# Stacked keys and doubled queries in the attention scores of one hybrid decoder layer, narrow key tiles with both heads in one bank, and a norm's mean placed between two projection tiles

## The chip, the cores and the metric

The kernel runs on one core of one Trainium2 chip. A core has five engines that work side by side, each through its own list of instructions, in order: PE (TensorE) multiplies matrices, DVE (VectorE) and ACT (ScalarE) work elementwise, POOL (GpSimd) does the same more slowly, and SP (SyncE) starts data transfers (DMAs). They wait for each other by semaphores. PE writes its results into PSUM, a small memory of eight banks of 128 partitions by 512 f32 values; everything else lies in SBUF, 128 partitions wide. The metric is the device time of one execution in microseconds; the lower the better.

## The reference

One layer of a decoder over 512 tokens of width 1024, in f32. What matters here is the first sublayer. From h = RMSNorm(x) one projection makes q, k, v (8 heads of 64), the inputs of a short convolution, and two gates. The heads do a causal "stick-breaking" attention:

```python
z = einsum('bhqd,bhkd->bhqk', qb, kb) / sqrt(64)          # scores
log_fail  = where(k_pos < q_pos, log_sigmoid(-z), 0)
log_later = cumsum(log_fail, reverse, over keys) - log_fail
weights   = where(k_pos < q_pos, exp(log_sigmoid(z) + log_later), 0)
out       = einsum('bhqk,bhkd->bhqd', weights, vb)
```

The convolution branch and the attention branch are projected, gated, added and projected again (x1 = x + ...). Then a cross-attention from RMSNorm(x1) into 256 memory tokens (4 heads of 256, softmax), then a SwiGLU feed-forward of width 2816, then a last norm.

## The kernel before, in words

Activations are held transposed (features on partitions, the 512 tokens along the row). Every f32 operand of a product is split into two parts of TensorE's f32r type, hi (a rounded copy, made by ACT) and lo (the rest, made by DVE: source minus hi). A product is three matmuls, hi*hi, hi*lo and lo*hi, added up in one PSUM bank (`mm3`, L153; the instructions of a projection carry the lines L154 to L156). A projection of 128 output features is 24 such matmuls of 512 columns (`gemm`, L158); the weights come through `load_w` (L137): SP loads 512 KB (`wr`), ACT makes `wh` (L149), DVE makes `wl` (L150), four buffers of each.

The attention runs over `steps`: four pairs of heads p, and in each the key tiles kt = 3, 2, 1, 0. A tile holds 128 keys on partitions and the queries that can see them along the row: `span(kt)` gives n = 256 columns for kt = 3 and kt = 2, 384 for kt = 1, 512 for kt = 0. One step has three parts, which the loop at L448 interleaves: `scores` of the next step, `weights` of this one and `values` of the one before.

- `qk_part` (L283) projects one of q and k for a pair of heads, scales it on DVE (L286, tile `qk`) and splits it (`split`, L168 and L169): head 0 on partitions 0 to 63, head 1 on 64 to 127.
- `scores` (L348): for each head its own PSUM bank z; three matmuls per head whose operands are 64 partitions high (L356), the two heads alternating. Then, per head, three ACT passes (L361 to L363: abs, exp, ln), one on DVE (L364), the causal mask on POOL (`causal`, L336), a split (`lsplit`, L344 and L345) and for kt of 2 and 1 the running sum over later keys (L373) and a second split.
- `weights` (L377): matmuls add the later keys' sums (L385, a matrix of -1) and the sums within the tile (L388, a triangle of -1) onto z in PSUM; ACT takes exp (L390), POOL masks, DVE makes the two parts `ah` and `al` (L394, L395).
- `values` (L399): four matmuls with v (L406). Here v is stored as hi in one half of the 128 columns and lo in the other, so two matmuls per head do.

Around these lies the `fill`: projections of the next heads, of the convolution and of the first gates, handed out over the 16 steps. Nothing in the code fixes the order within this stage on an engine: the framework orders the instructions of each engine from their priorities and a cost model when the program is built.

Later, at L605, the residual x1 is made with the sum of its squares (`squares_mean`, L176). `mean1[1]` (`turned`, L193) turns that sum into one reciprocal root per token: two matmuls with a matrix of 1/1024 (L185, tile `varb`), an ACT copy of one row (L196, `vrow`), two small DMAs that lay it out over partitions (L205, L207, `vr`), and six small operations (`rstd_of`, L116). The cross-attention's queries are `mem_q(h)` (L613), two projections of 24 matmuls (`mq`), made from the not yet normed x1 so that the mean isn't needed for them; `r1s` (L625) enters the softmax scale.

## Time and profile before

| | us |
|---|---|
| median of 3 runs (lowest, highest) | 860.55 (859.35, 860.62) |
| the profiled execution's own time | 860.42 |
| its span, first to last instruction | 858.7 |
| what lies around the span | 1.7 |

The stages along the span, by the trace: to 27 us the load of x and the projection of v; 27 to 207 us the attention with its fill; to 311 us gates and branches; to 356 us the memory's keys and values; to 400 us x1; to 463 us, overlapping, the cross-attention; to 516 us its output; 517 to 747 us the first and 747 to 843 us the second half of the feed-forward; then the last norm and the stores.

How the rows are read: a row of the timeline is start, length, engine, line, operation, output<-inputs, shapes, how many (x); brackets give the idle time before it and what ended that. Matmuls of PE overlap in their pipeline, so a length of 0.39 us is not the pace: the pace is the distance from one start to the next. A row x2 merges instructions that follow each other.

### The profile page before, as it was taken

The page shows a single profiled execution, that of the slowest core. Times are in us where ns is not written, and L with a number is a line of the kernel's source. Part 1 is how long each engine was busy: PE and PEld are TensorE (multiplying, and loading weights), DVE is VectorE, ACT ScalarE, POOL GpSimd, SP SyncE. Part 2 cuts the span into 40 slices and gives each one's busy share as a digit, 9 for nine tenths or more (in the row PEclk, how much of TensorE's full clock was granted, in tenths as well). Part 3 has the DMA queues.
Part 4 walks back from the last instruction along what each step waited for, and adds up shares of the span by engine and source line. Part 5 has one row for each costly group of instructions (what it writes and reads, how often), then busy time and mean ns, then how long its engine had stood idle before and what let it go on. Part 6 is the DMA issues. An engine that isn't in the chain of part 4 may idle for free.

```text
span 858.7 us, 12803 instructions
## 1 busy us (share of the span) xinstructions
PE 844.8 (98%) x4822; PEld 735.7 (86%) x4822; DVE 657.7 (77%) x1074; ACT 459.7 (54%) x843; POOL 153.7 (18%) x187
## 2 busy tenths in 40 slices
PE   9999999999999999999999999999999999999995
PEld 7788888877888899887888789999999999888884
DVE  7778888987665766577455678888888778999886
ACT  7466676665332354443444565655444555576654
POOL 0022221111566630064000011111111110000001
PEclk9999999999999999999999999999999999999998
DMA  8422212224578765466341325676676763465452
GB/s 295 138 96 86 87 63 73 74 75 172 217 284 305 285 235 193 172 245 241 107 130 50 92 69 148 175 191 175 182 186 178 189 187 88 155 224 199 163 179 98
DMA packets 49232, 139.55 MB, mean 163 GB/s; under 512 B 5265, under 2 KB 7313, under 8 KB 46354
## 3 DMA queue, kind: packets, MB, share of 16 engines
q1 hardware_dynamic: 39538, 103.83, 35.0%
q0 software_dynamic: 9344, 34.62, 15.4%
q8 instruction: 38, 0.62, 0.3%
q10 hardware_dynamic: 288, 0.28, 0.1%
q14 instruction: 24, 0.20, 0.1%
HBM read 125.07 MB, written 13.64 MB: 162 GB/s over the span
## 4 chain that ended last, share of the span: by engine, by line
PE 95%; DVE 3%; ACT 1%; issue 1%; POOL 0%; ACTq 0%; POOLq 0%
PE z L738 15%; PE p L1001 10%; PE pr L155 8%; PE pr L156 8%; PE pr L154 8%; PE y L738 7%; PE v L738 4%; PE r L154 3%; PE r L155 3%; PE r L156 3%; PE v L267 3%; PE br L154 2%; PE br L155 2%; PE br L156 2%; PE mq L156 2%; PE mq L154 2%
## 5 line engine op out<-in xcount | busy, mean ns | idle before, releaser
L149 ACT CAST wh<-wr 128x1024 fp32r<-128x1024 f32 x84 | 88.0, 1052 | 163.9 <-issue 71.2
L150 DVE TENSOR_TENSOR wl<-wr,wh 128x1024 fp32r<-128x1024 f32 x84 | 110.6, 1319 | 35.5 <-ACT wh L149 35.5
L155 PE MATMUL pr<-xgl,wh 128*128 128x512 f32 x288 | 112.4, 390 | 0.0
L156 PE MATMUL pr<-xgh,wl 128*128 128x512 f32 x288 | 112.3, 390 | 0.0
L154 PE MATMUL pr<-xgh,wh 128*128 128x512 f32 x288 | 112.2, 390 | 0.0
L478 POOL TENSOR_TENSOR pre<-pre 128x512 f32<-128x512 f32 x44 | 71.8, 1636 | 31.7 <-DMA pre<-in_w_ffn_out_dram 29.4
L707 POOL DMA_DIRECT2D ws<-in_w_ffn_in_dram x22 | 26.6, 1207 | 260.9 <-DVE wf L728 104.1
L738 PE MATMUL z<-xdh,wf 128*128 128x256 f32 x352 | 70.4, 283 | 0.2 <-ACT sb L759 0.2
L156 PEld LDWEIGHTS pr<-xgh,wl 128*128 128x128 f32 x288 | 54.1, 188 | 11.3
L154 PEld LDWEIGHTS pr<-xgh,wh 128*128 128x128 f32 x288 | 54.1, 188 | 11.1
L155 PEld LDWEIGHTS pr<-xgl,wh 128*128 128x128 f32 x288 | 54.1, 188 | 11.0
L759 ACT COPY sa<-z 128x256 f32<-128x256 f32 x44 | 16.4, 373 | 79.0 <-PE z L738 78.1
L738 PEld LDWEIGHTS z<-xdh,wf 128*128 128x128 f32 x352 | 57.9, 192 | 0.5 <-ACT sb L759 0.4
L728 DVE TENSOR_TENSOR wf<-s,wf 128x512 fp32r<-128x512 f32 x44 | 30.3, 691 | 25.8 <-ACT wf L727 25.7
L738 PE MATMUL z<-xdl,wf 128*128 128x256 f32 x176 | 49.8, 283 | 0.0
L819 DVE TENSOR_TENSOR wl<-wr,wh 128x1024 fp32r<-128x1024 f32 x33 | 40.3, 1220 | 5.1 <-ACT wh L886 5.1
L886 ACT CAST wh<-wr 128x1024 fp32r<-128x1024 f32 x33 | 34.6, 1049 | 5.7 <-ACT f01h L815 2.4
L738 PE MATMUL z<-xch,wf 128*128 128x256 f32 x176 | 35.4, 284 | 0.1
L738 PE MATMUL y<-xch,wf 128*128 128x256 f32 x176 | 35.4, 283 | 0.0
L738 PE MATMUL v<-xoh,wf 128*128 128x256 f32 x176 | 35.4, 283 | 0.0
L738 PE MATMUL z<-xf,wf 128*128 128x256 f32 x264 | 35.4, 283 | 0.0
L738 PE MATMUL y<-xoh,wf 128*128 128x256 f32 x176 | 35.3, 283 | 0.0
(332 smaller groups left out, 2417.0 us busy)
## 6 DMA issues: line engine op xcount, KB each, us to landing
wr<-in_w_in_dram SPq DMA_DIRECT2D x36, 512.0 KB, 3.3
pre<-in_w_ffn_out_dram POOLq DMA_DIRECT2D x11, 1024.0 KB, 8.2
sums<-pre POOLq DMA_DIRECT2D x11, 1024.0 KB, 5.1
ws<-in_w_ffn_in_dram SPq DMA_DIRECT2D x22, 512.0 KB, 3.7
wg<-in_w_ffn_in_dram SPq DMA_DIRECT2D x22, 512.0 KB, 4.1
ws<-in_w_ffn_in_dram POOLq DMA_DIRECT2D x22, 512.0 KB, 5.9
wr<-sums SPq DMA_DIRECT2D x22, 512.0 KB, 3.9
wr<-in_w_ffn_out_dram SPq DMA_DIRECT2D x16, 512.0 KB, 4.0
```

The source lines that it names most:

```text
L149: after(nc.scalar.copy(h2, raw), lead[-1:])
L150: lows.append(nc.vector.tensor_tensor(out=l2, in0=raw, in1=f(h2), op=ALU.subtract))
L154: nc.tensor.matmul(ps, a[0], b[0], start=start, stop=False, **kw)
L155: nc.tensor.matmul(ps, a[0], b[1], start=False, stop=False, **kw)
L156: nc.tensor.matmul(ps, a[1], b[0], start=False, stop=stop, **kw)
L478: nc.gpsimd.tensor_tensor(out=t[:, a, :], in0=t[:, a, :], in1=t[:, b, :], op=ALU.add)
L707: nc.gpsimd.dma_start(s13, a[:, 0:4:3, :], accum_op=ALU.add)
L728: nc.vector.tensor_tensor(out=w[:, 1, :], in0=raw, in1=f(w[:, 0, :]), op=ALU.subtract)
L738: nc.tensor.matmul(ps[:, :HS], a, b, start=i < 3 and k == 0 and j == 0, stop=k == KP - 1 and j == 2, skip_group_check=True)
L819: nc.vector.tensor_tensor(out=lo, in0=src, in1=f(hi), op=ALU.subtract)
L886: nc.scalar.copy(hi, raw)
L1001: nc.tensor.matmul(res[i][s2], a[:, ts], b, start=j == 0 and n == 0, stop=j == NJ - 1 and n == 2)
```

## The change

It has three parts.

1. Scores by full-height matmuls. For each head a tile `k` of 128 partitions holds the hi part of the head's keys on its own half and the lo part on the other half. For each head two tiles `q` hold the queries' hi part, and their lo part, on both halves. A matmul of `k` with the hi `q` gives hi*hi + lo*hi at once; with the lo `q` it gives hi*lo + lo*lo. So a head has two matmuls of 128 partitions where it had three of 64, and the product also holds the lo*lo term. ACT and DVE now write each half by itself: four half-high operations for k and four for q where there were two full ones each. DVE writes the lo part of k directly onto the other half; for q, four DMAs of SP's queue (64 partitions by 512 values, 128 KB) copy each half onto the other.
2. Narrow key tiles. For kt = 3 and kt = 2 the two heads' 256 columns lie side by side in one bank z (`heads_of`), and all that follows, on ACT, DVE, POOL and in the matmuls with the -1 matrices, takes 512 columns once, where it took 256 columns twice. The mask gets a pattern with a head dimension. The wider tiles kt = 1 and 0 stay with one bank per head, and read the narrow tile's sums by slices (`part_of`, `carried`).
3. The second norm's mean. `mean1[1]` is called between the two projections of `mem_q(0)` and no longer ahead of both.

```diff
--- before.py
+++ after.py
@@ -278,14 +278,35 @@
         gemm(ps, w, xg)
         return ps
 
-    qk = [[None] * 2 for _ in range(TT)]
+    qs, ks = {}, {}
+    HALVES = slice(0, HD), slice(HD, P)
 
     def qk_part(p, i):
+
+
         ps = project((O_Q, O_K)[i] + p * P)
         t = tmp("qk")
         nc.vector.scalar_tensor_tensor(out=t, in0=ps, scalar=(HD ** -0.5, 1.0)[i], in1=r0b,
                                        op0=ALU.mult, op1=ALU.mult)
-        qk[p][i] = split(t, "qk")
+        if i:
+            ks[p] = [unit("k") for _ in range(2)]
+            for h, hs in enumerate(HALVES):
+                casts.append(nc.scalar.copy(ks[p][h][hs, :], t[hs, :]))
+            for h, hs in enumerate(HALVES):
+                nc.vector.tensor_tensor(out=ks[p][h][HALVES[1 - h], :], in0=t[hs, :],
+                                        in1=f(ks[p][h][hs, :]), op=ALU.subtract)
+            return
+        qs[p] = [[unit("q") for _ in range(2)] for _ in range(2)]
+        for h, hs in enumerate(HALVES):
+            casts.append(nc.scalar.copy(qs[p][h][0][hs, :], t[hs, :]))
+        for h, hs in enumerate(HALVES):
+            hi, lo = qs[p][h]
+            nc.vector.tensor_tensor(out=lo[hs, :], in0=t[hs, :], in1=f(hi[hs, :]),
+                                    op=ALU.subtract)
+        for part in range(2):
+            for h, hs in enumerate(HALVES):
+                q = f(qs[p][h][part])
+                nc.sync.dma_start(q[HALVES[1 - h], :], q[hs, :])
 
     gates = {}
 
@@ -334,8 +355,16 @@
         return c0, S - c0, (kt + 1) * P - c0
 
     def causal(t, d):
-        nc.gpsimd.affine_select(out=t[:, :d], in_=t[:, :d], compare_op=ALU.is_gt, fill=0.0,
-                                base=P - d, pattern=[[1, d]], channel_multiplier=-1)
+        nc.gpsimd.affine_select(out=t[:, :, :d], in_=t[:, :, :d], compare_op=ALU.is_gt, fill=0.0,
+                                base=P - d, pattern=[[0, t.shape[1]], [1, d]],
+                                channel_multiplier=-1)
+
+    def heads_of(kt):
+
+        return ((0, 1),) if kt >= TT - 2 else ((0,), (1,))
+
+    def by_head(t, n):
+        return t.rearrange("p (h c) -> p h c", c=n)
 
     rest, later = {}, {}
 
@@ -345,56 +374,79 @@
         nc.vector.tensor_tensor(out=lo, in0=t, in1=f(hi), op=ALU.subtract)
         return hi, lo
 
+    def part_of(parts, hs, h, n):
+
+        i = hs.index(h)
+        return [t[:, i * n:(i + 1) * n] for t in parts]
+
     def scores(p, kt):
         c0, n, d = span(kt)
-        q, k = qk[p]
-        ks = slice(kt * P, (kt + 1) * P)
-        z2 = zs[p, kt] = [ztile("z") for _ in range(2)]
-        for i, (a, b) in enumerate(((0, 0), (0, 1), (1, 0))):
-            for h in range(2):
-                hs = slice(h * HD, (h + 1) * HD)
-                nc.tensor.matmul(z2[h][:, :n], k[a][hs, ks], q[b][hs, c0:],
-                                 start=i == 0, stop=i == 2)
-        for h in range(2):
-            z = z2[h][:, :n]
-            e = tmp("e")[:, :n]
+        keys = slice(kt * P, (kt + 1) * P)
+        zs[p, kt] = []
+        for hs in heads_of(kt):
+            bank = ztile("z")
+            zs[p, kt].append(bank)
+            for i, h in enumerate(hs):
+                for part in range(2):
+                    nc.tensor.matmul(bank[:, i * n:(i + 1) * n], ks[p][h][:, keys],
+                                     qs[p][h][part][:, c0:], start=i + part == 0, stop=part == 1,
+                                     skip_group_check=True)
+        for hs, bank in zip(heads_of(kt), zs[p, kt]):
+            w = len(hs) * n
+            z = bank[:, :w]
+            e = tmp("e")[:, :w]
             nc.scalar.activation(e, z, AF.Abs)
             nc.scalar.activation(e, e, AF.Exp, scale=-1.0)
             nc.scalar.activation(e, e, AF.Ln, bias=1.0)
             nc.vector.scalar_tensor_tensor(out=e, in0=z, scalar=0.0, in1=e, op0=ALU.max,
                                            op1=ALU.add)
-            causal(e, d)
-            sp[p, kt, h] = lsplit(e, n, f"l{kt}", 4)
+            causal(by_head(e, n), d)
+            bufs = 4 // len(hs)
+            sp[p, kt, hs] = lsplit(e, w, f"l{kt}", bufs)
             if kt == TT - 1:
-                later[h] = e
-                rest[p, kt - 1, h] = sp[p, kt, h]
+                later[hs] = e
+                rest[p, kt - 1, hs] = sp[p, kt, hs]
             elif kt > 0:
                 m = span(kt + 1)[0] - c0
-                nc.vector.tensor_tensor(out=e[:, m:], in0=e[:, m:], in1=later[h], op=ALU.add)
-                later[h] = e
-                rest[p, kt - 1, h] = lsplit(e, n, f"r{kt}", 4)
+                for before in heads_of(kt + 1):
+                    if before == hs:
+                        nc.vector.tensor_tensor(out=e, in0=e, in1=later[hs], op=ALU.add)
+                    elif hs[0] in before:
+                        old = part_of([later[before]], before, hs[0], n - m)[0]
+                        nc.vector.tensor_tensor(out=e[:, m:], in0=e[:, m:], in1=old, op=ALU.add)
+                later[hs] = e
+                rest[p, kt - 1, hs] = lsplit(e, w, f"r{kt}", bufs)
+
+    def carried(p, kt, hs):
+
+        if (p, kt, hs) in rest:
+            return rest[p, kt, hs]
+        n = span(kt + 1)[1]
+        return part_of(rest[p, kt, (0, 1)], (0, 1), hs[0], n)
 
     def weights(p, kt):
         c0, n, d = span(kt)
-        av[p, kt] = []
-        for h in range(2):
-            z = zs[p, kt][h][:, :n]
+        av[p, kt] = {}
+        for hs, bank in zip(heads_of(kt), zs[p, kt]):
+            w = len(hs) * n
+            z = bank[:, :w]
             if kt < TT - 1:
                 off = span(kt + 1)[0] - c0
-                for part in rest[p, kt, h]:
+                for part in carried(p, kt, hs):
                     nc.tensor.matmul(z[:, off:], neg1, part, start=False, stop=False,
                                      skip_group_check=True)
-            for part in sp[p, kt, h]:
+            for part in sp[p, kt, hs]:
                 nc.tensor.matmul(z, negtri, part, start=False, stop=True, skip_group_check=True)
-            a = tmp("a")[:, :n]
+            a = tmp("a")[:, :w]
             exps.append(nc.scalar.activation(a, z, AF.Exp))
-            causal(a, d)
-            ah, al = unit("ah")[:, :n], unit("al")[:, :n]
+            causal(by_head(a, n), d)
+            ah, al = unit("ah")[:, :w], unit("al")[:, :w]
             r = r0[:, kt:kt + 1]
             nc.vector.tensor_scalar(out=ah, in0=a, scalar1=r, scalar2=None, op0=ALU.mult)
             nc.vector.scalar_tensor_tensor(out=al, in0=a, scalar=r, in1=f(ah), op0=ALU.mult,
                                            op1=ALU.subtract)
-            av[p, kt].append((ah, al))
+            for h in hs:
+                av[p, kt][h] = part_of((ah, al), hs, h, n)
 
     def values(p, kt):
         c0 = span(kt)[0]
@@ -610,17 +662,20 @@
 
     om = []
 
-    def mem_q(h):
+    def mem_q(h, between=None):
         got = []
         for j in range(2):
+            if j and between:
+                between()
             w = load_w(wmq_d[2 * h + j])
             ps = mmtile("mq")
             gemm(ps, w, x1g)
             got.append(split(ps, "mq"))
         return got
 
-    r1 = mean1[1]("r1", log_exp_tables(sigmoid))
-    q_next = mem_q(0)
+    r1s = []
+    q_next = mem_q(0, lambda: r1s.append(mean1[1]("r1", log_exp_tables(sigmoid))))
+    r1 = r1s[0]
     r1s = cpool.tile([P, TT], F32, tag="r1s", name="r1s")
     nc.vector.tensor_scalar(out=r1s, in0=r1, scalar1=(D // MH) ** -0.5, scalar2=None, op0=ALU.mult)
     for h in range(MH):
```

The tables of the framework's order show it at three places. First PE in the attention, head pair p = 1: the scores of kt = 2 (z_975 and z_976 before, z_937 in the change) and the triangle sums of kt = 3 behind them. Before:

```order
L356 MATMUL z_975<-qkh_510,qkh_547 128x256
L356 MATMUL z_976<-qkh_510,qkh_547 128x256
L356 MATMUL z_975<-qkl_511,qkh_547 128x256
L356 MATMUL z_976<-qkl_511,qkh_547 128x256
L356 MATMUL z_975<-qkh_510,qkl_548 128x256
L356 MATMUL z_976<-qkh_510,qkl_548 128x256
L388 MATMUL z_884<-l_898,negtri 128x256
L388 MATMUL z_884<-l_899,negtri 128x256
L388 MATMUL z_885<-l_908,negtri 128x256
L388 MATMUL z_885<-l_909,negtri 128x256
```

And in the change, at the same place:

```order
L391 MATMUL z_937<-q_507,k_552 128x256
L391 MATMUL z_937<-q_508,k_552 128x256
L391 MATMUL z_937<-q_509,k_553 128x256
L391 MATMUL z_937<-q_510,k_553 128x256
L439 MATMUL z_857<-l_868,negtri 128x512
L439 MATMUL z_857<-l_869,negtri 128x512
```

Ten matmuls have become six; they stand, before and now, between a projection of 24 matmuls and the four matmuls of `values`.

Second PE at the second norm's mean, where `varb` is the mean, `mq` the first two query projections. Before:

```order
L155 MATMUL mq_3924<-xgl_3776,wh_3920 128x512
L185 MATMUL varb_3900<-acch_3864,mean_r 128x512
L156 MATMUL mq_3924<-xgh_3775,wl_3921 128x512
L154 MATMUL mq_3924<-xgh_3816,wh_3920 128x512
L155 MATMUL mq_3924<-xgl_3817,wh_3920 128x512
L185 MATMUL varb_3900<-accl_3865,mean_r 128x512
L156 MATMUL mq_3924<-xgh_3816,wl_3921 128x512
```

In the change:

```order
L154 MATMUL mq_3724<-xgh_3677,wh_3720 128x512
L155 MATMUL mq_3724<-xgl_3678,wh_3720 128x512
L156 MATMUL mq_3724<-xgh_3677,wl_3721 128x512
L185 MATMUL varb_3755<-acch_3684,mean_r 128x512
L185 MATMUL varb_3755<-accl_3685,mean_r 128x512
L154 MATMUL mq_3779<-xgh_3392,wh_3775 128x512
L155 MATMUL mq_3779<-xgl_3393,wh_3775 128x512
```

The mean's first matmul stood behind 17 of the first projection's 24 and its second four places later (three of `mq` between them); now both stand together behind all 24.

Third ACT at the same place (`wh` are weights' casts, `mqh` the two query tiles' hi parts, `ry` needs the DMA `vr`). Before:

```order
L196 COPY vrow_3899<-varb_3900 1x512
L149 CAST wh_4202<-wr_4200 128x1024
L168 CAST mqh_3949<-mq_3924 128x512
L149 CAST wh_4237<-wr_4235 128x1024
L123 ACTIVATE ry_3909<-vr_3906,eps_t 128x4
L168 CAST mqh_3984<-mq_3959 128x512
```

In the change:

```order
L149 CAST wh_4022<-wr_4020 128x1024
L168 CAST mqh_3749<-mq_3724 128x512
L196 COPY vrow_3754<-varb_3755 1x512
L149 CAST wh_4057<-wr_4055 128x1024
L123 ACTIVATE ry_3764<-vr_3761,eps_t 128x4
L168 CAST mqh_3804<-mq_3779 128x512
```

The row copy has moved behind a weight cast and the first query tile's cast; `ry` stands ahead of the second query tile's cast in both.

## The prediction, as put on record before the run

> **What bounds the kernel now.** I read the page's busy times and its chain of waits first, then the timeline of PE in the two stages that the change touches, then the groups of instructions there.
>
> ```profile
> PE 844.8 (98%) x4822; PEld 735.7 (86%) x4822; DVE 657.7 (77%) x1074; ACT 459.7 (54%) x843; POOL 153.7 (18%) x187
> PE 95%; DVE 3%; ACT 1%; issue 1%; POOL 0%; ACTq 0%; POOLq 0%
> ```
>
> PE is busy for 98% of the span and makes 95% of the chain that ends last. So a microsecond taken from PE's own list counts in full, as long as the others keep up, and one taken from ACT or DVE counts only where PE waits for it. But a busy PE isn't a PE at its pace. The pace has to be read from the distance between starts.
>
> **The scores.** PE around three score blocks, for 256, 384 and 512 columns, each behind the last matmul of a projection:
>
> ```profile
> 87.23 0.39 PE L156 MATMUL pr<-xgh,wl 128*128 128x512 f32 x1
> 87.55 0.38 PE L356 MATMUL z<-qkh,qkh 64*128 64x256 f32 x2
> 87.77 0.28 PE L356 MATMUL z<-qkl,qkh 64*128 64x256 f32 x2
> 87.89 0.28 PE L356 MATMUL z<-qkh,qkl 64*128 64x256 f32 x2
> 88.10 0.73 PE L388 MATMUL z<-l,negtri 128*128 128x256 f32 x4
> 88.67 0.40 PE L406 MATMUL o<-ah,v 128*128 128x512 f32 x1
> ...
> 57.24 0.39 PE L156 MATMUL pr<-xgh,wl 128*128 128x512 f32 x1
> ...
> 58.61 0.40 PE L388 MATMUL z<-l,negtri 128*128 128x256 f32 x2
> ...
> 70.47 0.39 PE L156 MATMUL pr<-xgh,wl 128*128 128x512 f32 x1
> ...
> 72.03 0.51 PE L388 MATMUL z<-l,negtri 128*128 128x384 f32 x2
> 72.37 0.40 PE L385 MATMUL z<-r,neg 128*128 128x256 f32 x2
> ```
>
> First the pace of full-height matmuls. From 399.99 to 403.62 us (rows below, the first and the 17th of a projection) 16 matmuls of 512 columns start: 3.63 / 16 = 0.227 us each. The 384 columns at 72.03 take 0.34 for two, 0.17 each. For 256 columns the chain gives
>
> ```profile
> 520.37 1.44 PE z L738 x12
> ```
>
> 0.12 us each. Now a score block. The two heads of a row x2 start together, so six half-high matmuls could pass in the time of three. They don't: the pairs at 87.55 and 87.89 hold PE for 0.22 and 0.21 us, only the middle one for 0.12. The rows at the borders are late as well: the projection's last matmul takes 0.32 us to the next start (its pace is 0.227), and the four triangle matmuls take 0.57 (their pace makes 0.48). Charged with all that, the scores of 256 columns cost 88.67 - 87.23 - 0.227 - 0.48 = 0.73 us. In the same way, with two -1 matmuls of 256 columns ahead of the row that ends the sum, 384 columns cost 58.61 - 57.24 - 0.227 - 0.24 = 0.90, and 512 cost 72.03 - 70.47 - 0.227 - 0.24 = 1.09. A pair of heads has 256 twice: 0.73 + 0.73 + 0.90 + 1.09 = 3.45, four pairs 13.8 us.
>
> The change has four full-height matmuls per block. Everywhere in these rows full height follows full height (triangle, then values, then projection) at its pace, whatever the operands, so I price them at 4 x 0.12, 4 x 0.17 and 4 x 0.227: 0.48 + 0.48 + 0.70 + 0.91 = 2.57 per pair, 10.3 in all. **Gain 3.5 us.** Bounds: if the borders' 0.09 + 0.09 us belonged to the change of operands and not of height, they'd stay, 16 x 0.18 = 2.9, and the gain would be 0.6; upward, rows rounded by 0.02 us in 16 blocks let it reach 3.8.
>
> The Trainium skill has a rule on each side. "TensorEngine Tiling (Array Packing)", Overview, says that contracting over 64 rows in two independent tiles gives up to 2x, which speaks against full height: by it the block costs three passes and the change adds a fourth. Its Key Properties say that changing the tiling mode drains TensorE. The trace agrees with the second, with 0.09 us at each border, and the first holds only for the middle pair. By the first alone the scores would go from 7.7 to 10.3 us.
>
> **The -1 matrices.** For kt = 3, two pairs of 256-column matmuls become two of 512, for kt = 2 four: 6 per pair of heads, 24 in all. Each replaces 0.240 by 0.227: **gain 0.3 us**; bounds 0 (DVE's lo part comes later) and 0.4.
>
> **The second norm's mean.** PE and DVE there:
>
> ```profile
> 399.99 0.39 PE L154 MATMUL mq<-xgh,wh 128*128 128x512 f32 x1
> 403.62 0.39 PE L155 MATMUL mq<-xgl,wh 128*128 128x512 f32 x1
> 405.19 0.43 DVE L179 CAST acch<-acc 128x512 fp32r<-128x512 f32 x1
> 405.65 0.69 DVE L180 TENSOR_TENSOR accl<-acc,acch 128x512 fp32r<-128x512 f32 x1
> 405.76 0.47 PE L185 MATMUL varb<-acch,mean_r 128*128 128x512 f32 x1 [1.75 <-DVE acch L179]
> 406.06 0.40 PE L156 MATMUL mq<-xgh,wl 128*128 128x512 f32 x1
> ```
>
> The mean's first matmul stands in the middle of a projection and waits for `acch`: 405.76 - 403.62 - 0.227 = 1.91 us, the longest wait of PE behind its start. In the change all 24 matmuls pass first, to 399.99 + 24 x 0.227 = 405.43. `acch` lets the mean start at 405.76 as before: 0.33 lost. But its second matmul now follows at once and needs `accl`, which ends at 406.34; with the same 0.1 us of signal PE has it at 406.45 where the next start in that place was 406.06: 0.39 lost. That leaves 1.91 - 0.72 = 1.19 us gained. What is late next is the chain behind it:
>
> ```profile
> 407.19 0.58 ACT L196 COPY vrow<-varb 1x512 f32<-1x512 f32 x1 [4.99 <-PE varb L185]
> 413.36 1.05 ACT L149 CAST wh<-wr 128x1024 fp32r<-128x1024 f32 x1 [3.90 <-issue]
> 413.85 0.17 DVE L124 TENSOR_SCALAR rv<-vr 128x4 f32<-128x4 f32 x1 [3.01 <-DMA vr<-row]
> 414.51 0.56 ACT L168 CAST mqh<-mq 128x512 fp32r<-128x512 f32 x1
> 415.13 0.39 PE L154 MATMUL sc<-kmh,mqh 128*128 128x256 f32 x1
> ```
>
> From the end of the row copy (407.77) to the landed `vr` (413.85) go 6.08 us in two DMAs. In the change the copy stands behind a weight cast (1.05) and the first query tile's cast (0.58), which start when PE's 23rd matmul has left the first tile's `wh`, at 399.99 + 22 x 0.227 + 0.39 = 405.4. So the copy runs from 407.0 to 407.6, and `vr` is there at 413.7. Behind `vr` on ACT stand `ry` (now 0.1 us between the cast's end at 414.41 and `mqh`, say 0.2) and then the second `mqh` (0.56), done at 414.5. PE, 1.19 us ahead, wants it at 415.13 - 1.19 = 413.9. So about half of a microsecond comes back there: **gain 0.7 us**, between 0 (the DMAs land later) and 1.2. DVE holds the second tile's lo part behind `rv` in the same way, but PE uses it only later, behind more of `mq`.
>
> **What the others must carry.** ACT and DVE get two half-high pieces for each full one:
>
> ```profile
> L414 ACT COPY ot<-o 64x512 f32<-64x512 f32 x8 | 4.7, 582 | 0.3
> L415 DVE TENSOR_TENSOR ot<-o,ot 64x512 f32<-64x512 f32 x8 | 5.5, 687 | 0.7 <-ACT ot L414 0.5
> L344 ACT CAST l<-e 128x256 fp32r<-128x256 f32 x16 | 6.5, 407 | 5.7 <-POOL e L337 5.5
> L344 ACT CAST l<-e 128x512 fp32r<-128x512 f32 x8 | 5.0, 622 | 0.9 <-POOL e L337 0.8
> L345 DVE TENSOR_TENSOR l<-e,l 128x256 fp32r<-128x256 f32 x16 | 6.7, 422 | 0.8 <-ACT l L344 0.8
> L345 DVE TENSOR_TENSOR l<-e,l 128x512 fp32r<-128x512 f32 x8 | 5.6, 696 | 0.5 <-ACT l L344 0.5
> ```
>
> Half the partitions save nothing (582 and 687 ns), so with one more piece in each of 8 projections DVE pays 8 x 0.69 = 5.5 us more and ACT 8 x 0.58 = 4.6 at most. The narrow tiles pay it back: a 512 for two 256 saves 0.15 us on DVE and 0.19 on ACT in these rows, and by the code a head has 4 DVE and 5 ACT operations of 256 columns at kt = 3, 6 and 6 at kt = 2. Over eight heads that makes 40 pairs on DVE and 44 on ACT: 6 and 8 us. Both engines come out a little lighter. The chain behind a narrow z gets no longer: one head's chain used to run after the other's, and three ACT passes of 0.6 replace six of 0.4. Slack is there:
>
> ```profile
> 86.45 0.42 DVE L345 TENSOR_TENSOR l<-e,l 128x256 fp32r<-128x256 f32 x1
> ```
>
> That last part ends at 86.87; PE uses it in the fourth triangle matmul, at about 88.5: 1.6 us. POOL's mask over two heads isn't in the trace; between the mask of 256 columns
>
> ```profile
> L337 POOL TENSOR_SCALAR_AFFINE_SELECT e<-e 128x256 f32<-128x256 f32 x8 | 3.3, 420 | 9.7 <-DVE e L364 9.7
> L478 POOL TENSOR_TENSOR pre<-pre 128x512 f32<-128x512 f32 x44 | 71.8, 1636 | 31.7 <-DMA pre<-in_w_ffn_out_dram 29.4
> ```
>
> and the slowest POOL pass of 512 I take 0.6, near the first since it is the same operation; 1.6 would eat 1.1 of the slack.
>
> The q copies stand in SP's queue, and the weight loads behind them wait until DVE has made the lo halves, some 1.4 us more. SP's own waits say what that is worth:
>
> ```profile
> SPq L141 <- DVE wl L150: 362.2, 69, 11.7
> wr<-in_w_in_dram SPq DMA_DIRECT2D x36, 512.0 KB, 3.3
> ```
>
> SP waits for free buffers, not the data for SP: loads run far ahead of PE, so I cost this at nothing; without that cover it would be 4 x 1.4 = 5.6 us. Only the first pair of heads needs its copies soon. A copy isn't in the trace; by weight loads of 512 KB it lands within 3.3 us (bound upward), and its order on PE has been put six matmuls later than the first score stood. I take 0.1 us, at most 1.5.
>
> **Sum.** 860.42 - 3.5 - 0.3 - 0.7 + 0.1 = 856.0 us for an execution like the profiled one, which lies 0.13 us under the median shown: I predict 856.0.
>
> **Rivals.**
>
> - *Borders stay* (6%). The 0.09 us at each border come with new operands. For it: they stand where q and k come in. Against: triangle to values to projection changes operands too, without any. The scores then gain 0.6: 860.42 - 0.6 - 0.3 - 0.7 = 858.8.
> - *A fourth pass* (4%), on the other side. If the late pairs and borders are the price of q and k as operands and not of half height, a block pays 0.73 - 0.36 = 0.37 beside its passes also at full height, and the passes go from three to four: 0.12 + 0.12 + 0.17 + 0.23 = 0.64 per pair of heads, 2.6 us more. 860.42 + 2.6 - 1.0 = 862.0. It decides once a full-height block keeps over 0.22 us (3.5 / 16) of the extra. The Trainium skill's "TensorEngine Tiling (Array Packing)", Overview, would expect the fourth pass. Against the rest of it: the triangle and values matmuls change operand and bank as often and keep their pace.
> - *New waits in the narrow steps* (13%). POOL's longer mask and DVE's order make PE wait some 0.3 us in each of 8 narrow steps: 856.0 + 2.4 = 858.4. For it: DVE is the busiest after PE. Against: the 1.6 us of slack.
> - *The mean's wait only moves* (12%): the two DMAs take as long and ACT holds the second `mqh` for all of it; 856.0 + 0.7 = 856.7.
> - *More comes off* (5%): PE's other short waits in the attention shrink too, 854.5.
>
> **How the numbers follow.** The forecast has the rest, 60%. About 0.2% is what a measurement of this kernel can tell from no change, 1.7 us: below 858.8 is faster, over 862.3 slower. "Borders stay" falls on the first limit, half to each side; of the new waits a fifth passes it; the fourth pass lies close under the second limit. So faster 0.89, same 0.08, slower 0.03. The range from 854.0 to 858.6 takes in the bounds of the mean's term (0 to 1.2), the first copies and the new waits.
>
> **What would show it.** Right: full-height score blocks of 0.48, 0.70 and 0.91 us with the projection's last matmul before them at 0.23 to the next start; the 1.75 us wait at `varb` down to under half a microsecond and a new wait of about that size at `sc` for `mqh`; PE's busy time shorter by about 3 to 4 us and its count by 56. Wrong: idle PE in front of the triangle or value matmuls of kt = 3 and 2, SP waits that end in casts of `wh`, or starts in the score blocks further apart than the pace.

## The result, and the profile after

| | before | after |
|---|---|---|
| median of the four runs taken together (us) | 860.23 (859.35 to 860.62) | 856.29 (854.92 to 856.82) |
| the profiled execution's own time | 860.42 | 856.12 |
| its span | 858.7 | 854.4 |

The ratio is 0.9953, 95% interval 0.9936 to 0.9970: faster by 3.9 us, where 4.4 were forecast (856.0). One of the ten executions of experiment 6 ran at a granted clock of 0.85 and took 924.27 us; its ratio leaves it out. The predicted time is right to 0.3 us, but its parts are not all right: one term came out at twice its size, and two losses that the forecast didn't have made up for it. That the total agrees so closely is in part luck.

The page of the changed kernel, its busy times and the head of its chain of waits:

```profile
PE 841.8 (99%) x4766; PEld 738.1 (86%) x4766; DVE 662.7 (78%) x1042; ACT 460.2 (54%) x807; POOL 154.4 (18%) x171
PE 93%; DVE 4%; ACT 1%; issue 1%; POOL 0%; ACTq 0%; POOLq 0%
```

PE has 56 matmuls and 3.0 us of busy time less and still bounds the kernel. DVE's share of the chain rose from 3 to 4%. To see where the time was won, the same matmul is looked up in both timelines. Here is the first matmul of the first query projection, the first of the branches (all of the attention but its last values matmuls lies ahead of it), and the first cross-attention score; first before:

```profile
27.80 0.40 PE L154 MATMUL pr<-xgh,wh 128*128 128x512 f32 x1
...
200.04 0.39 PE L154 MATMUL br<-oh,wh 128*128 128x512 f32 x1
...
413.34 0.28 PE L154 MATMUL sc<-kmh,mqh 128*128 128x256 f32 x1
```

and after:

```profile
28.14 0.40 PE L154 MATMUL pr<-xgh,wh 128*128 128x512 f32 x1
...
196.84 0.39 PE L154 MATMUL br<-oh,wh 128*128 128x512 f32 x1
...
408.66 0.28 PE L154 MATMUL sc<-kmh,mqh 128*128 128x256 f32 x1
```

The changed kernel starts its attention 0.34 us late, ends it 3.20 early, and is 4.68 us ahead at the scores behind the second norm's mean. So the attention gave 3.54 us and the mean 1.48 (between the two, from 204 to 400 us of the span before, the lead stays at 3.20); 0.34 were lost ahead of both, in the part ahead of the attention, which the change doesn't touch, and 4.3 are left at the end of the span, so 0.4 were lost behind.

| part | forecast | in the profiled executions |
|---|---|---|
| attention (scores, -1 matrices, first copies) | 3.5 + 0.3 - 0.1 = 3.7 | 3.54 |
| second norm's mean | 0.7 | 1.48 |
| start | 0 | -0.34 |
| behind the scores | 0 | -0.4 |
| sum | 4.4 | 4.3 |

Two of the blocks that answer to the three shown of before, for 256 and for 512 columns:

```profile
86.32 0.39 PE L156 MATMUL pr<-xgh,wl 128*128 128x512 f32 x1
86.54 0.63 PE L391 MATMUL z<-q,k 128*128 128x256 f32 x4
87.01 0.62 PE L439 MATMUL z<-l,negtri 128*128 128x512 f32 x2
87.47 0.39 PE L458 MATMUL o<-ah,v 128*128 128x512 f32 x1
...
70.03 0.39 PE L156 MATMUL pr<-xgh,wl 128*128 128x512 f32 x1
70.26 1.08 PE L391 MATMUL z<-q,k 128*128 128x512 f32 x4
71.17 0.39 PE L436 MATMUL z<-r,neg 128*128 128x256 f32 x2
```

Four full-height matmuls hold PE for 0.47 and 0.91 us; the block of 384 columns, from 57.25 to 57.95, for 0.70. The projection ahead of them goes on to the next start in 0.22 or 0.23, and the triangle matmuls behind take 0.46 for two: no border is left. And the second norm's mean, with what feeds it and what follows:

```profile
402.00 0.39 PE L156 MATMUL mq<-xgh,wl 128*128 128x512 f32 x1
402.11 0.69 DVE L180 TENSOR_TENSOR accl<-acc,acch 128x512 fp32r<-128x512 f32 x1
402.22 0.47 PE L185 MATMUL varb<-acch,mean_r 128*128 128x512 f32 x1
402.86 0.50 PE L185 MATMUL varb<-accl,mean_r 128*128 128x512 f32 x1 [0.16 <-DVE accl L180]
...
403.67 0.57 ACT L196 COPY vrow<-varb 1x512 f32<-1x512 f32 x1
404.27 0.31 SPq L205 DMA_DIRECT2D row<-vrow  x1
404.68 0.36 SPq L141 DMA_DIRECT2D wr<-in_w_mem_o_dram  x1
405.44 0.38 SPq L207 DMA_DIRECT2D vr<-row  x1
408.36 0.17 DVE L124 TENSOR_SCALAR rv<-vr 128x4 f32<-128x4 f32 x1 [3.21 <-DMA vr<-row]
```

The mean's first matmul no longer waits for `acch`, since the last query matmul starts at 402.00 and the mean 0.22 later; only its second one stands, for `accl`, 402.86 - 402.22 - 0.227 = 0.41 us. `vr` has landed at 408.36, 4.12 us after the row copy's end at 404.24 and ahead of the first score at 408.66. No score waits for a query cast behind it.

### The profile page after: what moved, and what is told of

The parts are those of the page before. It is cut to its first block, busy times and chain, and to the rows that moved or that the text cites. A ratio compares the mean times of both kernels' runs of the same rounds, so it can differ in the third digit from the quotient of the medians.

```text
span 854.4 us, 12626 instructions
## 1 busy us (share of the span) xinstructions
PE 841.8 (99%) x4766; PEld 738.1 (86%) x4766; DVE 662.7 (78%) x1042; ACT 460.2 (54%) x807; POOL 154.4 (18%) x171
## 4 chain that ended last, share of the span: by engine, by line
PE 93%; DVE 4%; ACT 1%; issue 1%; POOL 0%; ACTq 0%; POOLq 0%
PE z L793 15%; PE p L1056 10%; PE pr L154 7%; PE pr L155 7%; PE pr L156 7%; PE y L793 7%; PE v L793 4%; PE r L154 3%; PE r L155 3%; PE r L156 3%; PE v L267 3%; PE br L154 2%; PE br L156 2%; PE br L155 2%; PE mq L156 1%; PE mq L154 1%
## 5 line engine op out<-in xcount | busy, mean ns | idle before, releaser
L150 DVE TENSOR_TENSOR wl<-wr,wh 128x1024 fp32r<-128x1024 f32 x84 | 111.9, 1334 | 33.3 <-ACT wh L149 33.1
```

The lines of the kernel that those rows point to most:

```text
L150: lows.append(nc.vector.tensor_tensor(out=l2, in0=raw, in1=f(h2), op=ALU.subtract))
```

## The experiments

Nine runs follow in eight experiments; one of them is the change again. The kernel before stood at 860.1 to 860.3 us beside each set; ratios are to it.

**1. The mean alone.** The kernel before, with this one edit:

```diff
-    r1 = mean1[1]("r1", log_exp_tables(sigmoid))
-    q_next = mem_q(0)
+    r1s = []
+    q_next = mem_q(0, lambda: r1s.append(mean1[1]("r1", log_exp_tables(sigmoid))))
+    r1 = r1s[0]
```

> The kernel before with only the second norm's mean moved between the two query tiles; scores and narrow tiles as before. Theory (the 6.08 us from row copy to landed vr held a stand of SP's queue behind a weight load that waits for a free buffer, and in the changed order that load no longer waits): the mean's wait falls from 1.91 to about 0.4 us, vr lands about 4 to 4.5 us after the row copy's end, sc does not wait for the query cast, gain 1.5 us: about 858.7. Rival 1 (as predicted: the two DMAs take 6 us by themselves and sc waits): gain 0.7, 859.5. Rival 2 (the 1.5 us came from the lighter attention, which moved PE and the weight loads against each other): gain under 0.5, 859.8 or more.

Measured: 858.88 us, ratio 0.9987 (0.9978 to 0.9996), 1.1 us faster with an interval from 0.3 to 1.9. The time by itself doesn't separate 0.7 from 1.5; the trace does. SP's queue, and the first operation that has `vr`:

```profile
407.99 0.31 SPq L205 DMA_DIRECT2D row<-vrow  x1
...
409.15 0.38 SPq L207 DMA_DIRECT2D vr<-row  x1
...
412.16 0.17 DVE L124 TENSOR_SCALAR rv<-vr 128x4 f32<-128x4 f32 x1 [3.30 <-DMA vr<-row]
```

The weight load goes out between them at 408.39. `vr` is there 4.20 us after the row copy's end (407.96), as in the full change, and no score waits behind it. The wait at the mean fell from 1.91 to 0.40 us. From the start of the attention to the first score this execution gains 1.48 us on the kernel before. So the mean's 1.5 us come without the lighter attention, and both rivals fall.

**2. Why `vr` came late.** The kernel before, with the row's two DMAs on other queues than SP's:

```diff
-            return rstd_of(turned_row(row[0:1, :n * P], n, "v" + s, nc.sync, nc.sync), n, s, tables)
+            return rstd_of(turned_row(row[0:1, :n * P], n, "v" + s, nc.scalar, nc.gpsimd), n, s, tables)
```

> The kernel before with the second norm's row stored by ACT's queue and vr loaded by POOL's, so that no weight load of SP stands between the two; everything else as before. Theory (2.5 us of the 6.08 from the row copy's end to the landed vr is SP's queue, which stands at a weight load until DVE frees its buffer): vr lands some 3.5 to 4.5 us after the row copy's end, by 412.3 instead of 413.9. Since the mean's own wait of 1.9 us is untouched, the time stays within 0.3 us of the kernel before. Rival (the two DMAs take their 6 us on any queue): vr at 413.5 to 414.2.

Measured: 860.41 us, ratio 1.0003 (0.9993 to 1.0013), no difference.

```profile
407.43 0.58 ACT L196 COPY vrow<-varb 1x512 f32<-1x512 f32 x1 [4.67 <-PE varb L185]
...
409.47 0.77 POOL L207 DMA_DIRECT2D vr<-row  x1 [4.38 <-DMA row<-vrow]
412.02 0.17 DVE L124 TENSOR_SCALAR rv<-vr 128x4 f32<-128x4 f32 x1 [0.67 <-DMA vr<-row]
```

From the copy's end at 408.01 to `vr` go 4.01 us in place of 6.08, so the two DMAs don't take 6 us by themselves. The time stays the same since PE's wait at the mean is untouched. SP's own rows in the kernel before say where the other two were:

```profile
407.79 0.31 SPq L205 DMA_DIRECT2D row<-vrow  x1
410.26 0.35 SPq L141 DMA_DIRECT2D wr<-in_w_mem_o_dram  x1
410.66 0.42 SPq L207 DMA_DIRECT2D vr<-row  x1
```

There SP stood from 408.1 to 410.26 at a weight load between the row's two DMAs. In the change that load goes out 0.1 us behind the row, at 404.68, since the work on the weights that frees its buffer (ACT's wh, then DVE's wl, which ends at 404.55) now comes ahead of the row copy; in the kernel before, that wl ended at 410.23.

**3. Without the common bank.** The changed kernel with one bank per head at every key tile (and, in the running sum, the slice `e[:, m:]` that this needs):

```diff
-        return ((0, 1),) if kt >= TT - 2 else ((0,), (1,))
+        return (0,), (1,)
```

> The changed kernel without the narrow tiles' common bank: each head keeps its bank, its three ACT passes and its mask at every key tile, as in the kernel before; full-height scores and the moved mean stay. Theory (scores 3.1 to 3.3 us, mean 1.5, merged -1 matrices 0.3, the narrow tiles otherwise free): 0.3 us over the change plus what DVE and ACT, now with 6 and 8 us more work, make PE wait, 856.6 to 857.3. Rival 1 (the common bank costs waits at masks and triangle matmuls that the merged -1 matrices only pay back): equal to the change or up to 0.5 us under it, 855.8 to 856.3. Rival 2 (the common bank is needed: DVE at 78% can't carry half pieces and split narrow tiles together): over 858.

Measured: 856.91 us, ratio 0.9961 (0.9949 to 0.9974); the change's own interval overlaps with it, so by the times alone the common bank can't be told from nothing. In the trace PE has waits that the change doesn't have or has shorter (its last row is the memory norm's mean):

```profile
107.17 0.73 PE L391 MATMUL z<-q,k 128*128 128x512 f32 x2 [0.40 <-ACT a L442]
...
174.69 0.35 PE L185 MATMUL varb<-acch,mean_r 128*128 128x256 f32 x1 [0.64 <-DVE ot L468]
```

Between the same two matmuls as above (27.38 to 197.46 us here) its attention gains 2.2 us over the kernel before, not 3.54 (3.53 in a second profile of the change, from experiment 8). In this execution the rest came back elsewhere: 0.76 at the start, which no edit touches, and 0.4 at the second norm's mean, where `accl` happened to be ready. So the common bank is worth about 1.4 us in the attention in these executions, of which at most 0.2 are the merged -1 and triangle matmuls; the rest is work that DVE and ACT no longer have to do in time. The time lies where the theory had it; the first rival, that the common bank costs waits, falls by the trace, and the second, over 858 us, by the time.

**4. One mask or two.** The changed kernel with POOL's mask of a narrow tile once per head:

```diff
-        nc.gpsimd.affine_select(out=t[:, :, :d], in_=t[:, :, :d], compare_op=ALU.is_gt, fill=0.0,
-                                base=P - d, pattern=[[0, t.shape[1]], [1, d]],
-                                channel_multiplier=-1)
+        for h in range(t.shape[1]):
+            nc.gpsimd.affine_select(out=t[:, h, :d], in_=t[:, h, :d], compare_op=ALU.is_gt,
+                                    fill=0.0, base=P - d, pattern=[[1, d]],
+                                    channel_multiplier=-1)
```

> The changed kernel with POOL's mask of a narrow tile as two operations, one per head, in place of one over both; the order on PE, ACT and DVE is the same. Theory (a mask's length is set by what DVE does beside it: 0.59 to 0.70 us for most, 1.08 and 1.48 us beside two longer DVE operations): the two parts take 0.42 each or more, nothing is gained, within 0.3 us of the change. Rival (the one pass over two heads of 256 columns is what collides with DVE and delays the memory norm's mean, which waits 0.47 us): the wait falls to 0.2, 0.3 to 0.5 us under the change.

Measured: 856.75 us, ratio 0.9961 (0.9949 to 0.9974), nothing gained; the median is 0.5 us over the change's, a little more than expected, and the intervals overlap. The group of POOL's masks after exp at kt = 3, of the change:

```profile
L358 POOL TENSOR_SCALAR_AFFINE_SELECT a<-a 128x512 f32<-128x512 f32 x4 | 3.4, 854 | 24.1 <-ACT a L441 24.1
```

and of this run:

```profile
L359 POOL TENSOR_SCALAR_AFFINE_SELECT a<-a 128x256 f32<-128x256 f32 x8 | 4.6, 595 | 23.1 <-ACT a L442 23.1
```

Over the four steps the masks per head take 4.6 us where one over both heads took 3.4, and PE's wait at the memory norm's mean is 0.64 us where it was 0.47 in the change: longer, not shorter. The rival falls, and splitting the mask brings nothing.

**5. A third full-height pass.**

```diff
-                for part in range(2):
+                for j, part in enumerate((0, 1, 1)):
                     nc.tensor.matmul(bank[:, i * n:(i + 1) * n], ks[p][h][:, keys],
-                                     qs[p][h][part][:, c0:], start=i + part == 0, stop=part == 1,
+                                     qs[p][h][part][:, c0:], start=i + j == 0, stop=j == 2,
```

> The changed kernel with a third full-height matmul per head and block: the low query half is multiplied and added twice, so the scores are off by that correction, and each block has six full-height matmuls where the kernel before had six of half height. Theory (full height costs only its pace, 0.12, 0.17 and 0.227 us a matmul; borders are gone): 2 more matmuls a block, (0.24 + 0.24 + 0.34 + 0.454) x 4 = 5.1 us over the change, 861.4, so about 1.2 us over the kernel before: the half height's two tiles had saved 1.5 us of the 3 passes that they could. Rival (borders or late pairs come with q and k as operands): a block's extra shows beside the pace and the rise is more than 5.1; or PE had hidden waits in the blocks that a third pass covers, and the rise is under 4.5 us.

Measured: 861.24 us, ratio 1.0013 (1.0004 to 1.0021), so 5.0 us over the change where 5.1 were expected. A block of 256 columns:

```profile
87.81 0.87 PE L391 MATMUL z<-q,k 128*128 128x256 f32 x6
88.53 0.74 PE L439 MATMUL z<-l,negtri 128*128 128x512 f32 x2
```

Six full-height matmuls take 0.72 us, six times 0.12. With the 0.73 of the six half-height ones before, that looks as if the half height had overlapped nothing. The next two runs show that this reading is wrong.

**6. Heads one after the other.** The kernel before with its loops over heads and over terms exchanged:

```diff
-        for i, (a, b) in enumerate(((0, 0), (0, 1), (1, 0))):
-            for h in range(2):
+        for h in range(2):
+            for i, (a, b) in enumerate(((0, 0), (0, 1), (1, 0))):
```

> The kernel before with the half-height scores in another order: the three matmuls of head 0, then the three of head 1, in place of the two heads by turns; the same matmuls, banks and results. Theory (two heads overlap when they stand by turns, and each border of full and half height costs about 0.09 us): six single passes and two borders, 0.72 + 0.18 = 0.90 for 256 columns where it was 0.73, 1.20 for 384 where it was 0.90, 1.54 for 512 where it was 1.09: 1.1 us a pair of heads more, about 864.6. Rival 1 (the turns of two heads overlap nothing but the middle pair, and cost as much by themselves): 0.72, 1.02 and 1.36 a block, some 2 us more, 862. Rival 2 (no overlap anywhere): no difference, 860.2.

Measured: 861.50 us, ratio 1.0014 (1.0004 to 1.0023). The block that answers to the first one of the prediction:

```profile
87.38 0.39 PE L156 MATMUL pr<-xgh,wl 128*128 128x512 f32 x1
87.69 0.39 PE L356 MATMUL z<-qkh,qkh 64*128 64x256 f32 x2
87.92 0.29 PE L356 MATMUL z<-qkl,qkh 64*128 64x256 f32 x2
88.03 0.28 PE L356 MATMUL z<-qkh,qkl 64*128 64x256 f32 x2
...
88.82 0.40 PE L406 MATMUL o<-ah,v 128*128 128x512 f32 x1
```

The program now issues three matmuls of head 0 and then three of head 1, and still each pair of heads starts together (head 1 some 0.01 us behind head 0, where it was 0.003), and the block takes 1.44 us from the projection's last start to the values' first, as before (88.67 - 87.23). None of the three expectations had that: whatever their order, the pairs of two heads go side by side, and the order costs nothing in a block. The 1.4 us more come from elsewhere, 0.9 of them from a longer wait at the memory norm's mean (PE goes from 173.18 to 174.49 here, from 172.98 to 173.41 before).

**7. Six pairs in a row.** The kernel before with its two correction terms again:

```diff
-        for i, (a, b) in enumerate(((0, 0), (0, 1), (1, 0))):
+        for i, (a, b) in enumerate(((0, 0), (0, 1), (1, 0), (0, 1), (1, 0), (0, 1))):
```

> The kernel before with three more half-height matmuls per head and block: the two low-half products are added again (one of them twice), so the scores are off by these corrections, and a block has six pairs of heads in a row in place of three. Theory (two heads always overlap, and a block pays 0.37 us for coming from full height and going back, whatever its length): three pairs at the full-height pace more, 0.36 for 256 columns, 0.51 for 384, 0.68 for 512, so blocks of 1.09, 1.41 and 1.77, 1.9 us a pair of heads and 7.7 in all: 867.8. Rival 1 (the late pairs, 0.22 in place of 0.12, belong to each change of operands): 0.1 more for two of three added pairs, 3.2 us in all beside it, 871. Rival 2 (the two heads do not overlap when pairs stand longer in a row): six passes of 0.12 more a block, over 875.

Measured: 869.02 us in two executions, ratio 1.0102 (1.0017 to 1.0187); the profiled one took 867.34, the other 870.70. These times can't tell the theory's 867.8 from the first rival's 871; the trace can:

```profile
89.36 0.39 PE L156 MATMUL pr<-xgh,wl 128*128 128x512 f32 x1
89.67 0.39 PE L356 MATMUL z<-qkh,qkh 64*128 64x256 f32 x2
89.90 0.28 PE L356 MATMUL z<-qkl,qkh 64*128 64x256 f32 x2
...
90.37 0.28 PE L356 MATMUL z<-qkl,qkh 64*128 64x256 f32 x2
90.57 0.74 PE L388 MATMUL z<-l,negtri 128*128 128x256 f32 x4
91.15 0.40 PE L406 MATMUL o<-ah,v 128*128 128x512 f32 x1
```

The second to the sixth pair start 0.12 us apart (90.37 - 89.90 for four), twelve half-height matmuls in the time of six. What is late is the same as with three pairs: 0.31 in place of 0.227 ahead of the first pair, 0.23 in place of 0.12 behind it, 0.20 in place of 0.12 behind the last, and 0.58 for the four triangle matmuls, whose pace makes 0.48. From the projection's last start to the values' first go 1.79 us, 0.35 more than with three pairs: three passes of 0.12. Only the way in and the way out of half height cost something, and both rivals fall.

**8. Both means without their waits.** What the trace of the change left standing: 0.41 us for `accl` at the second norm's mean, and 0.47 us at the memory norm's mean, whose bank belongs to the values and is freed late. The edit moves the first behind one k (three matmuls) of the second query tile and gives the other a bank of the scores' pool:

```diff
-                rmb = mean[0]("rmb")
+                rmb = mean[0]("rmb", bank=ztile)
...
-            if j and between:
-                between()
             w = load_w(wmq_d[2 * h + j])
             ps = mmtile("mq")
-            gemm(ps, w, x1g)
+            for k in range(KD):
+                if j and between and k == 1:
+                    between()
+                mm3(ps, (w[0][:, k, :], w[1][:, k, :]), x1g[k], k == 0, k == KD - 1)
```

> The changed kernel with two edits at its means. The second norm's mean stands three matmuls (one k of the second query tile) later; the memory norm's mean goes to a bank of the scores' pool in place of one of the values' pool, and by that 12 matmuls earlier in PE's order. Theory (the 0.41 us at the second norm's mean is DVE's low part, which three matmuls of 0.227 cover; the 0.47 us at the memory norm's mean is a bank that DVE's last head operation frees late): both waits go to under 0.1 us, 0.7 to 0.9 us under the change. Rival (the wait moves on: the row copy, vr and the scaled queries come 0.7 us later and sc waits; a z bank is missed by the scores): the same as the change within 0.3 us, or slower.

Measured: 854.66 us (854.23 to 855.97), ratio 0.9944 (0.9931 to 0.9956). The change itself ran in the same set, for comparison:

> The changed kernel itself on the chip of this set, as the measure for the run with the later means: all theories 856.0 to 856.8.

856.19 us (854.76 to 856.52), ratio 0.9955 (0.9942 to 0.9967). In the trace of the run with the later means both waits are gone; at the second norm the two matmuls follow at the pace:

```profile
401.82 0.39 PE L185 MATMUL varb<-acch,mean_r 128*128 128x512 f32 x1
402.05 0.39 PE L185 MATMUL varb<-accl,mean_r 128*128 128x512 f32 x1
402.28 0.40 PE L154 MATMUL mq<-xgh,wh 128*128 128x512 f32 x1
```

Between the start of the attention and the first score this execution gains 0.9 us on the change; the medians lie 1.5 apart, with ranges and intervals that overlap. The theory's 0.7 to 0.9 us stand in the trace. It is the fastest of the kernels that ran, and clearly faster than the kernel before; that it beats the change is likely, and shown only in the trace.

## Why the prediction was right or wrong

**The scores (3.5 us): the gain and its cause right, one reading wrong.** The blocks came out at the predicted 0.48, 0.70 and 0.91 us (0.47, 0.70 and 0.92 by unrounded starts), and the projection ahead of them at its pace. The prediction wrote that six half-high matmuls could pass in the time of three, but don't. They do: experiments 6 and 7 show the two heads side by side in every pair. What made a block of before cost 0.73 is three passes of 0.12 and 0.37 for going to half height and back (0.39 and 0.41 for 384 and 512 columns), and that is the same for a block of three pairs and one of six. The price of four full-height passes was right because full height drops the 0.37, whatever its cause. Four passes against three cost one pass more, 0.12 to 0.227, and so every block gains 0.37 to 0.41 less one pass. The rule of the Trainium skill that the prediction set against the change ("TensorEngine Tiling (Array Packing)", Overview, up to twice the rate for 64 rows) is borne out by the trace within a run of half-height matmuls, at 0.12 us a pair. The same page's drain at a change of mode (Key Properties) fits the 0.37 us for the way there and back, by which that gain was lost here; the runs show this price and that it belongs to half height, not that it is a drain.

Counted with unrounded starts, from the matmul ahead of a block to the first projection behind it, the 16 blocks take 3.66 us less. At most 0.2 of that are the merged -1 matrices, so the scores gave about 3.5, as forecast. This includes the first block, which stays 0.47 us over the pace, in two pieces that wait for k's parts (0.80 over it in the kernel before), and two blocks of 256 columns that now wait 0.1 each at the triangle. The longer wait at the memory norm's mean, below, takes 0.27 off the attention's gain again.

**The -1 matrices (0.3 us).** Not separable in a time. By unrounded starts two matmuls of 256 columns take 0.235 us and one of 512 takes 0.227 to 0.232, so the merging gives 0.2 at most; the 0.3 came from a pace rounded to 0.12. What the common bank is worth is more than its matmuls: without it the attention lost 1.4 us, and experiment 3 shows PE waiting for ACT and DVE then. The prediction set the narrow tiles' savings on these engines against the half pieces' work, and did not ask what the half pieces would cost *without* them.

**ACT and DVE: both sides mis-sized, at little cost.** Both were to come out a little lighter. In the attention DVE's busy time went from 144.9 to 146.6 us and ACT's from 112.4 to 113.0. What PE waits longer for them is told below. Experiment 3, which has the half pieces without the common bank, separates the two sides: 151.6 on DVE and 117.4 on ACT. The half pieces cost 6.7 and 5.0 us (forecast 5.5 and at most 4.6), and the common bank gave back 5.0 and 4.4, not 6 and 8. The forecast had added up the lengths of single operations. But two of them in a row overlap in the trace, as here in the kernel before:

```profile
82.47 0.76 DVE L364 SCALAR_TENSOR_TENSOR e<-z,e 128x256 f32<-128x256 f32 x2 [0.56 <-ACT e L363]
L364 DVE SCALAR_TENSOR_TENSOR e<-z,e 128x512 f32<-128x512 f32 x8 | 5.2, 686 | 2.4 <-ACT e L363 2.4
```

Two operations of 0.42 us take 0.76 together, so one of 0.69 in their place saves 0.07, not 0.15.

**The new waits.** The memory norm's mean waits 0.47 us, where it waited 0.20 before. Ahead of it in time stand a mask and a DVE operation that are both long:

```profile
167.29 1.48 POOL L358 TENSOR_SCALAR_AFFINE_SELECT a<-a 128x512 f32<-128x512 f32 x1 [2.85 <-ACT a L441]
168.21 1.11 DVE L169 TENSOR_TENSOR yl<-gb,yh 128x512 fp32r<-128x512 f32 x1
...
170.37 0.39 PE L185 MATMUL varb<-acch,mean_r 128*128 128x256 f32 x1 [0.31 <-DVE ot L467]
```

The mask had been taken at 0.6 us, and by the single rows of the trace five of the eight over 512 columns take 0.62 to 0.70, the others 0.80, 1.08 and 1.48. That this one and DVE's 1.11 (0.69 elsewhere) lengthen the mean's wait is not shown: the wait was 0.64 with a mask per head (experiment 4) and 0.80 without the common bank (experiment 3). What it does wait for is the bank that DVE frees, since another bank, 12 matmuls earlier in PE's order, took the wait away (experiment 8). The "new waits in the narrow steps" rival was right in kind, with 0.27 + 0.2 us in all, not 2.4.

**The second norm's mean (0.7 us): mis-sized, 1.48.** The loss at `accl` came out at 0.41 (forecast 0.39), and the 0.33 at `acch` fell away, since DVE was that much earlier against PE: a weight operation ahead of it (L150) took 1.42 us, here and with the mean alone, where it had taken 1.75. The step that failed is the one that took the 6.08 us from the row copy to `vr` for "two DMAs". Two of these 6.08 us are a stand of SP's queue, and the row that shows it, the weight load at 410.26 between the row's two DMAs, could have been read in the trace of before. The new wait at `sc` that the prediction announced isn't there, in the change or with the mean alone. The rival "the mean's wait only moves" falls with it.

**The copies of q.** They land 2.4 us after their issue in the median, 2.2 to 3.9 in all, so the bound of 3.3 us was too low for some:

```profile
q<-q SPq DMA_DIRECT2D x16, 128.0 KB, 2.4
```

SP stands 25.5 us in all at them, for ACT's hi halves, and still PE has no wait for a weight in the attention. The first block is no worse than before: the lead of the changed kernel grows by 0.23 us from the projection ahead of it to the one behind it.

**The rivals with PE.** "Borders stay" (858.8) falls by the blocks; "a fourth pass" (862.0) too: with a third pass per head a block still takes exactly its six passes.

**What was not in the sum.** The start was 0.34 us later. The same projection starts at 27.38 us without the common bank, at 27.80 before, at 28.14 in the change and at 27.88 in the change's second profile, so this is a difference between executions. Behind the scores 0.4 us were lost; 0.29 of them are one wait for a weight's low part at 803 us. It was 0.55 in the change's second profile, 1.0 with the mask per head and absent in the eight other profiles. So it varies, but that the change makes it likelier is neither shown nor excluded. These two losses hid the 0.8 us by which the mean's term was too small.

## What to carry to other kernels

Going from full to half height on TensorE and back cost a fixed amount here (0.37 us for 256 columns), and inside a half-height run two heads shared each pass. So count the passes saved per visit. Three pairs saved one pass against four stacked full-height matmuls, 0.12 to 0.227 us, which is less. Six pairs against eight would save two, by these numbers (an estimate) 0.24 us for 256 columns and 0.45 for 512, against 0.37 and 0.41.

When a value has to pass through two small DMAs, read the queue's own rows between them. Here a weight load that waited for a buffer held the row's second DMA behind it in that queue, and moving the chain to a point where that buffer is free took this stand of 2 us away as well.

Where an edit adds work to one engine and another edit takes it off again, price each without the other, and price two short operations in a row by the time that they take together.

## What the runs showed of the hardware

The order of issue among half-height matmuls didn't matter: three of one head and then three of the other ran in pairs, the second and third starting 0.23 and 0.11 us behind the one ahead of it (0.22 and 0.12 by turns). The Trainium skill ("TensorEngine Tiling (Array Packing)", Key Properties) says that tiles operate independently; the trace agrees.

POOL's mask over 512 columns took between 0.62 and 1.48 us, the longest (1.47 and 1.48 again in two more profiles) beside two long DVE operations with two inputs, one of which was itself 1.11 in place of 0.69. The Trainium skill ("SBUF — State Buffer", SBUF: two separate sides) describes a port pair that VectorE and GpSimd share, held by one of them at a time; the rows agree: the mask that starts at 167.29 ends at 168.77, half a microsecond behind the end of the weight operation (168.29) that it met, and DVE's next one ends 0.55 behind the mask. No run here took the one away from beside the other, so this cause is argued, not shown.
